# Prompt attention on one NeuronCore: where the masks are added to the scores, and which operand of the compressed scores stands still

## Chip, core and metric

The kernel runs on one core of one Trainium2 chip. The metric is the time of one execution on the device in microseconds (us). An execution under the hardware profiler gives the trace; its times carry the argument.

## What is computed

One step of a hybrid decoder layer: a prompt of 1024 positions, and 8 sequences that each decode one token. One normalized input feeds three groups of heads: NSA attention (8 query heads of 64, 2 key/value heads, and three branches: compressed, selected, window), an RWKV-7 recurrence, and attention into 256 memory tokens. Their gated outputs go through one output projection. The change concerns the prompt's NSA attention, for which the reference says:

```python
def masked_softmax(s, mask):
    s = jnp.where(mask, s.astype(jnp.float32), -jnp.inf)
    m = jnp.max(s, axis=-1, keepdims=True)
    m = jnp.where(jnp.isfinite(m), m, 0.0)
    p = jnp.exp(s - m)
    return p / jnp.maximum(jnp.sum(p, axis=-1, keepdims=True), 1e-30)
...
    s = jnp.einsum('qghd,cgd->qghc', qg, ck) * SCALE
    valid = cend[None, :] <= qpos[:, None]
    p = masked_softmax(s, valid[:, None, None, :])
...
    mask = (kpos[None, :] <= qpos[:, None]) & (kpos[None, :] > qpos[:, None] - WINDOW) & (kpos[None, :] >= 0)
    p = masked_softmax(s, mask[:, None, None, :])
```

With 1024 positions the 16 selected blocks of 64 are all blocks, so the selected branch is plain causal attention. The window has 512 positions. The compressed branch has 63 keys, each over 32 rows at a stride of 16, and a query sees those that end at or before it.

## The kernel before

The program has three phases: projections, the recurrence and the tables of the prompt (0 to about 518 us), prompt attention (518 to 838), and the output projection with the NSA attention of the decoded tokens (838 to 1001). The change lies in the second; its tables are made in the first, in `prompt_cmp` (L1172).

Prompt attention takes the queries in 8 tiles of 128, from tile i = 7 down to tile 0. Tile i sees n1 = 128(i+1) keys. A **unit** (i, g, hp) is two heads of key/value group g. `attn_scores` (L1300) computes it for two branches: b = 0 (selected, all n1 keys) and b = 1 (window, the last five blocks of 128). Scores are products in a rounded float format with the keys split in a high and a low part (kh and kl), per piece of up to 512 keys, with the queries as the stationary operand (the weights). For i >= 4 ("split") every head has a PSUM tile p_s of its own, 1024 wide; for i < 4 two heads share one. There are 64 split heads and branches, and 64 others in 32 pairs.

- Masks: `add` (L1323) adds them on TensorE as identity products. `bmask` holds two 128x128 masks as weights, `identb` (a bf16 identity) is the other operand. The last 128 keys get the diagonal mask, and for split tiles the first block of the window gets another. There are 160 such products.
- VectorE then searches the row maximum, negated: nm (L1337 for one head, L1345 for two at a time). ScalarE computes exp(score + nm) from PSUM into SBUF, p, with the row sum (L1338, L1347). VectorE forms the factor fac (L1348, L1349), and GpSimd scales p by it (L1352).
- `pt_copy` transposes p by blocks on TensorE (p_pT), and ScalarE and VectorE take turns copying the result to SBUF (pt, L1296 and L1298). `attn_out` multiplies by the values into p_o (L1385 takes it into cat).

`attn_cmp` (L1241) does the compressed branch once per tile: for each g the 64-column compressed keys ckh and ckl stand still and 512 query columns (4 heads) move; a mask cmask goes in by identb; ScalarE copies the result (sc, L1253); four transposes (p_sq) turn it, so that queries lie on the partitions; then VectorE and ScalarE do the softmax (pcq, L1261 to L1273) and pcq is transposed for the values.

**Order.** The program is written out in one order: scores of a unit are issued two units ahead of their use. Side work (queries of the next tile, memory attention, the decoded tokens' RWKV step in `sample_rwkv`) is woven between the steps. A modelled clock on TensorE's instructions paces it: every matmul and transpose adds its modelled time (a mask product adds 0.118 us), each side step states when it may go on, and each tile has a rate:

```python
        us = max(n, 256) * 4.6e-4 if x.dtype != F32 else max(n, 64) * 1.7e-3
        self.clock += us * self.rows / 128
...
            def slot():
                for j in (3, 2, 1, 0):
                    spent[j] = min(spent[j] + rate[j], 3.0)
                    while spent[j] >= 1 and self.te.clock >= ready[j]:
                        step(j)
```

PSUM has two p_s tiles, three tiles that p_pT, p_q, p_sc and p_sq share, and one p_o. p has buffers for two units. SyncE issues nearly all transfers.

Of the kernel before, what the change touches and what calls it, by code (L numbers as in the profile page):

```python
# [23 lines left out]
NEG = -1.0e30  # L24
# [24 lines left out]
def bc(ap, shape):  # L49
    return ap.to_broadcast(shape)  # L50
# [64 lines left out]
class Step:  # L115
# [1004 lines left out]
    def key_pools(self):  # L1120
        tc = self.tc
        self.kctx = ExitStack()
        R = lambda c, name, bufs: c.enter_context(tc.tile_pool(name=name, bufs=bufs, reuse_waits="tile", side="right"))
        self.catp = R(self.octx, "catp", 1)
        self.k1p = R(self.octx, "keys1", 1)
        self.kh, self.kl, self.vs = [], [], []
        self.cs2 = R(self.octx, "cs2", 1)
        self.key_tiles(R(self.kctx, "keys0", 1))
        self.key_tiles(self.k1p)
        self.kt = R(self.kctx, "keyst", 1)  # L1130
        self.ckh = self.kt.tile([128, 1, 128], F32R, name="ckh")
        self.ckl = self.kt.tile([128, 1, 128], F32R, name="ckl")
        self.cvk = self.kt.tile([128, 2, 64], F32, name="cvk")
        self.bmask = self.kt.tile([128, 2, 128], BF, name="bmask")
        self.identb = self.kt.tile([128, 128], BF, name="identb")
        self.qs, self.pcT, self.y_rw, self.turn, self.cat = {}, {}, {}, 0, {}

    def key_tiles(self, pool):
# [33 lines left out]
    def prompt_cmp(self):  # L1172
        nc, I, O = self.nc, self.I, self.O
        V, A, G, PE = nc.vector, nc.scalar, nc.gpsimd, nc.tensor
        am = self.wk.tile([128, 256], F32, name="c_am", tag="sc")
        nc.sync.dma_start(am[:], I["c_at"][:, 0:256])
        V.tensor_copy(self.bmask[:].rearrange("p a b -> p (a b)"), am[:])
        V.tensor_copy(self.identb[:], self.ident[:])
        self.cmask = self.kt.tile([128, 8, 128], BF, name="cmask")
        am = self.slot(4, [128, 1024], F32, "c_am")  # L1180
        nc.sync.dma_start(am[:], I["c_at"][:, 256:1280])
        V.tensor_copy(self.cmask[:].rearrange("p i c -> p (i c)"), am[:])
# [118 lines left out]
    def attn_scores(self, i, g, hp, Ps):  # L1301
# [9 lines left out]
        sm = self.small.tile([128, 2, 2], F32, name="sm")  # L1311

        def scores(ps, q, b, c0, c1):
            w = c1 - c0
            masks = [(w - 128, 0)] if c1 == n1 else []
            if b == 1 and split and c0 == w0:
                masks.append((0, 1))
            u, o = c0 // 512, c0 % 512
            PE.matmul(ps, q, self.kh[u][:, 2 * b + g, o:o + w], start=True, stop=False)
            PE.matmul(ps, q, self.kl[u][:, 2 * b + g, o:o + w], start=False, stop=not masks)  # L1320
            return [(ps[:, o:o + 128], m, k == len(masks) - 1) for k, (o, m) in enumerate(masks)]

        def add(masks):  # L1323
            for ps, m, stop in masks:
                PE.matmul(ps, self.identb[:], self.bmask[:, m, :], start=False, stop=stop)

        f = self.small.tile([128, 2, 2], F32, name="fac")
        hd = 4 * g + 2 * hp
        for b in range(2):
            c0 = w0 if b else 0  # L1330
            for h in range(2):
                Ps[h, b] = self.pp.tile([128, 1024 if b == 0 else 640], F32, name="p", tag=f"p{b}")
            if split:
                for h in range(2):
                    ps = self.pS.tile([128, 1024], F32, name="p_s", tag="s")
                    add(scores(ps[:, c0:512], qs[:, hd + h, :], b, c0, 512) + scores(ps[:, 512:n1], qs[:, hd + h, :], b, 512, n1))
                    V.tensor_reduce(nm[:, h, b:b + 1], ps[:, c0:n1], axis=AX.X, op=OP.max, negate=True)  # L1337
                    A.activation(Ps[h, b][:, :n1 - c0], ps[:, c0:n1], AF.Exp, bias=nm[:, h, b:b + 1],  # L1338
                                 accum_out=sm[:, h, b:b + 1])
# [9 lines left out]
            V.reciprocal(f[:, :, b], f[:, :, b])  # L1349
# [265 lines left out]
    def sample_setup(self):  # L1615
# [683 lines left out]
def host_consts():  # L2299
# [73 lines left out]
```

## Time and profile before

| | us |
|---|---|
| median of 3 runs | 1003.12 (1000.74 to 1004.17) |
| the profiled execution | 1003.45, span of the trace 1001.1, granted TensorE clock 0.991 |
| ScalarE: exponents L1338, 64 | 55.7, mean 873 ns |
| VectorE: reduces L1337, 64 | 57.6, mean 918 ns |
| VectorE: reduces L1345, 32 | 25.6 |
| GpSimd: scaling L1352, 128 | 211.5, mean 1666 ns |
| TensorE: mask products, 160 | 25.9, mean 0.16 a product |
| ScalarE: copies L1253 of compressed scores, 16 | 9.4, mean 589 ns |

A row of groups names a line, an engine, an operation, what it writes and reads, and a count; then busy time, mean duration, and the engine's idle time ahead of it with what ended it. On TensorE matmuls overlap, and their ends are modelled, so what one costs is read between the starts of its neighbours. The prediction below shows the rows that it uses.

### The profile page before, as it was taken

How to read it: one execution, taken by the hardware profiler on the slowest of the kernel's cores; microseconds unless marked ns; L12 is line 12 of the kernel's file. 1: busy time of each engine (PE TensorE's matmuls, PEld its weight loads, DVE VectorE, ACT ScalarE, POOL GpSimd, SP SyncE). 2: the span in 40 equal slices, each digit the busy share in tenths (PEclk: the TensorE clock that was granted, in tenths of full speed). 3: DMA queues.
4: the chain of work that ended last, by engine and by line, in shares of the span. 5: the costliest groups of instructions: out<-in, count | busy, mean ns of one | idle time of the engine just before them, and what ended most of it. 6: DMA issues, size and time to landing. Idle time of an engine off the chain costs nothing.

```text
span 1001.1 us, 24786 instructions
## 1 busy us (share of the span) xinstructions
PE 948.8 (95%) x9955; PEld 788.9 (79%) x9955; DVE 681.4 (68%) x1954; ACT 446.8 (45%) x1005; POOL 254.0 (25%) x221
## 2 busy tenths in 40 slices
PE   7999999999999998999987999999999988998997
PEld 7998888878887887788865777887878876877874
DVE  6759589756684997633548677676869986357364
ACT  6754224223522432224436656665476665224212
POOL 2000000000000000000008776766578853112010
PEclk9999999999999999999999999999999999999999
DMA  8321313212321162265255223411200064984412
GB/s 283 95 75 40 90 34 117 76 45 74 85 77 34 49 178 67 61 158 135 81 159 171 86 81 116 149 43 45 59 22 16 28 149 130 324 276 160 158 65 76
DMA packets 133978, 104.20 MB, mean 104 GB/s; under 512 B 34593, under 2 KB 121128, under 8 KB 133736
## 3 DMA queue, kind: packets, MB, share of 16 engines
q1 hardware_dynamic: 128904, 90.92, 30.8%
q0 software_dynamic: 3200, 10.49, 3.0%
q8 instruction: 78, 1.28, 0.5%
q10 hardware_dynamic: 1760, 1.21, 0.4%
q14 instruction: 36, 0.29, 0.1%
HBM read 84.00 MB, written 22.78 MB: 107 GB/s over the span
## 4 chain that ended last, share of the span: by engine, by line
PE 65%; DVE 18%; ACT 6%; issue 4%; DMA 3%; POOL 2%; SPq 2%; ACTq 0%; DVEq 0%; POOLq 0%
PE p_pr L87 20%; PE p_pr L284 8%; PE p_out L87 5%; PE p_s L87 4%; PE p_pT L87 4%; PE p_o L87 3%; ACT p L1338 2%; POOL p L1352 2%; PE p_iy L87 2%; DVE nm L1337 1%; PE p_hid L87 1%; PE p_z L87 1%; PE p_it L87 1%; ACT p L1347 1%; DVE pt L1298 1%
## 5 line engine op out<-in xcount | busy, mean ns | idle before, releaser
L1352 POOL TENSOR_SCALAR p<-p,fac 128x640 f32<-128x640 f32 (+7 forms) x128 | 211.5, 1666 | 89.6 <-DVE fac L1349 34.6
L87 PE MATMUL p_pr<-h,whi 128*128 128x512 f32 (+5 forms) x928 | 231.0, 340 | 0.3 <-issue 0.3
L87 PEld LDWEIGHTS p_pr<-h,whi 128*128 128x128 f32 (+1 forms) x928 | 147.3, 184 | 19.0 <-issue 3.0
L87 PE MATMUL p_pr<-h,wlo 128*128 128x512 f32 (+5 forms) x464 | 152.5, 329 | 0.0
L999 POOL MEMSET w2d<- 128x128 f32 x1 | 0.2, 205 | 399.8 <-PE p_yy L87 399.8
L87 PEld LDWEIGHTS p_pr<-h,wlo 128*128 128x128 f32 (+1 forms) x464 | 85.1, 183 | 9.7
L284 PE MATMUL p_pr<-h,whi 128*128 128x256 f32 (+2 forms) x416 | 88.3, 308 | 0.4 <-DVE h L233 0.4
L87 PE MATMUL p_pT<-ident,p 128*128 128x128 f32 x528 | 72.8, 280 | 7.0 <-POOL p L1352 3.5
L87 PE MATMUL p_s<-kh,qs 128*128 128x512 f32 (+3 forms) x191 | 71.1, 380 | 1.9 <-ACT p L1338 1.8
L87 PEld LDWEIGHTS p_pT<-ident,p 128*128 128x128 f32 x528 | 56.8, 140 | 19.6 <-issue 7.1
L87 PE MATMUL p_o<-pt,vs 128*64 128x128 f32 x1056 | 70.0, 282 | 1.1 <-DVE c_r L1272 0.7
L1338 ACT ACTIVATE p<-p_s,nm 128x640 f32<-128x640 f32 (+3 forms) x64 | 55.7, 873 | 32.6 <-DVE nm L1337 26.2
L284 PEld LDWEIGHTS p_pr<-h,whi 128*128 128x128 f32 x416 | 67.4, 192 | 3.6 <-DVE h L233 0.6
L1337 DVE TENSOR_REDUCE nm<-p_s 128x1 f32<-128x640 f32 (+3 forms) x64 | 57.6, 918 | 14.9 <-PE p_s L87 14.9
L274 DVE TENSOR_TENSOR wlo<-wraw,whi 128x1024 fp32r<-128x1024 f32 (+1 forms) x34 | 40.7, 1197 | 35.2 <-ACT whi L273 35.1
L87 PEld LDWEIGHTS p_o<-pt,vs 128*64 128x64 f32 x1056 | 59.0, 140 | 6.7 <-issue 2.7
L284 PE MATMUL p_pr<-h,wlo 128*128 128x256 f32 (+2 forms) x208 | 63.3, 306 | 0.0
L87 PE MATMUL p_s<-kl,qs 128*128 128x512 f32 (+3 forms) x192 | 61.7, 338 | 0.0
L273 ACT ACTIVATE whi<-wraw 128x1024 fp32r<-128x1024 f32 (+1 forms) x35 | 36.4, 1039 | 50.9 <-PE p_pr L87 36.8
L1298 DVE COPY pt<-p_pT 128x512 f32<-128x512 f32 (+1 forms) x72 | 47.8, 670 | 16.2 <-PE p_pT L87 15.9
L1296 ACT ACTIVATE pt<-p_pT 128x512 f32<-128x512 f32 (+1 forms) x72 | 42.1, 587 | 27.6 <-PE p_pT L87 27.2
L87 PE MATMUL p_out<-woh,chi 128*128 128x512 f32 x128 | 52.5, 410 | 0.8 <-ACT woh L2194 0.6
(539 smaller groups left out, 2005.2 us busy)
## 6 DMA issues: line engine op xcount, KB each, us to landing
wraw<-in_w_in_dram SPq DMA_DIRECT2D x34, 512.0 KB
pg<-in_c_pool_dram SPq DMA_DIRECT2D x40, 256.0 KB
pg<-in_c_pool_dram SPq DMA_DIRECT2D x48, 128.0 KB
x<-in_x_prompt_dram SPq DMA_DIRECT2D x8, 512.0 KB
z_d<-zt SPq DMA_DIRECT2D x16, 256.0 KB
cat<-z_d SPq DMA_DIRECT2D x8, 512.0 KB
xres<-in_x_prompt_dram POOLq DMA_DIRECT2D x16, 256.0 KB, 3.8
wor<-in_w_out_dram SPq DMA_DIRECT2D x16, 256.0 KB
```

The lines of the kernel that those rows point to most:

```text
L87: self.last = getattr(self.engine, op)(*a, **k)
L273: nc.scalar.activation(hi[:, :, :n], raw[:, :, :n], AF.Copy)
L274: (low or nc.vector).tensor_tensor(lo[:, :, :n], raw[:, :, :n], hi[:, :, :n].bitcast(F32), op=OP.subtract)
L284: self.last_mm = self.pe.matmul(ps[:m, :b - a], w[:, k, :m], h[k][:, a:b], start=(k == 0 and i == 0), stop=(k == 7 and i == 2))
L999: nc.gpsimd.memset(w2d[:], 0.0)
L1296: nc.scalar.activation(pt[:, :n], ps[:, :n], AF.Copy)
L1298: nc.vector.tensor_copy(pt[:, :n], ps[:, :n])
L1337: V.tensor_reduce(nm[:, h, b:b + 1], ps[:, c0:n1], axis=AX.X, op=OP.max, negate=True)
L1338: A.activation(Ps[h, b][:, :n1 - c0], ps[:, c0:n1], AF.Exp, bias=nm[:, h, b:b + 1], accum_out=sm[:, h, b:b + 1])
L1347: A.activation(Ps[h, b][:, :n1], ps[:, h, :n1], AF.Exp, bias=nm[:, h, b:b + 1], accum_out=sm[:, h, b:b + 1])
L1352: nc.gpsimd.tensor_scalar(x, x, f[:, h, b:b + 1], None, op0=OP.mult)
```

## The change

`weigh` takes the place of the identity products, of the reduces and of ScalarE's reading of PSUM. bmask is now one row of masks, 128x1152: an "after" block, 896 columns of zeros and the diagonal block. Its last w columns are the mask of w keys; two pieces of 320 at a distance of 832 make the window's mask. One VectorE operation per head writes -(score + mask) to p in SBUF and keeps the row's minimum, which is the negated maximum; ScalarE then takes the exponent in place with scale -1.

```diff
-                    add(scores(ps[:, c0:512], qs[:, hd + h, :], b, c0, 512) + scores(ps[:, 512:n1], qs[:, hd + h, :], b, 512, n1))
-                    V.tensor_reduce(nm[:, h, b:b + 1], ps[:, c0:n1], axis=AX.X, op=OP.max, negate=True)
-                    A.activation(Ps[h, b][:, :n1 - c0], ps[:, c0:n1], AF.Exp, bias=nm[:, h, b:b + 1],
-                                 accum_out=sm[:, h, b:b + 1])
+                    scores(ps[:, c0:512], qs[:, hd + h, :], b, c0, 512)
+                    scores(ps[:, 512:n1], qs[:, hd + h, :], b, 512, n1)
+                    weigh(ps[:, c0:n1], h, b, c0)
...
-                add([m for h in range(2) for m in scores(ps[:, h, :n1], qs[:, hd + h, :], b, 0, n1)])
-                V.tensor_reduce(nm[:, :, b], ps[:, :, :n1], axis=AX.X, op=OP.max, negate=True)
                 for h in range(2):
-                    A.activation(Ps[h, b][:, :n1], ps[:, h, :n1], AF.Exp, bias=nm[:, h, b:b + 1], accum_out=sm[:, h, b:b + 1])
+                    scores(ps[:, h, :n1], qs[:, hd + h, :], b, 0, n1)
+                for h in range(2):
+                    weigh(ps[:, h, :n1], h, b, 0)
...
+        def weigh(ps, h, b, c0):
+            x, w = Ps[h, b][:, :n1 - c0], n1 - c0
+            if b == 1 and split:
+                m = bass.AP(tensor=self.bmask.tensor, offset=self.bmask.offset, ap=[self.bmask.ap[0], [832, 2], [1, 320]])
+                halves = lambda t: t.rearrange("p (a c) -> p a c", a=2)
+            else:
+                m, halves = self.bmask[:, 1152 - w:1152], lambda t: t
+            V.tensor_tensor_reduce(halves(x), halves(ps), m, -1.0, 3.0e38, op0=OP.add, op1=OP.min, accum_out=nm[:, h, b:b + 1])
+            A.activation(x, x, AF.Exp, scale=-1.0, bias=nm[:, h, b:b + 1], accum_out=sm[:, h, b:b + 1])
```

In `attn_cmp` the queries of one head stand still, and 64 compressed keys of one group move: 16 products into one PSUM tile that has queries on its partitions from the start, after one product that adds the mask for all heads. The copies sc and the transposes p_sq are gone.

```diff
-        for g in range(2):
-            pc = self.pM.tile([128, 4, 128], F32, name="p_sc", tag="m")
-            for n, ck in enumerate((self.ckh, self.ckl)):
-                PE.matmul(pc[:], ck[:, 0, :], qs[:, 4 * g:4 * g + 4, :], start=(n == 0), stop=False)
-            PE.matmul(pc[:], self.identb[:], bc(self.cmask[:, i:i + 1, :], [128, 4, 128]), start=False, stop=True)
-            A.activation(sc[g * 64:(g + 1) * 64], pc[g * 64:(g + 1) * 64], AF.Copy)
-            yield 0.5 + 2 * g
-        p2 = self.pM.tile([128, 4, 2, 64], F32, name="p_sq", tag="m")
+        p2 = self.pM.tile([128, 4, 2, 64], F32, name="p_sc", tag="m")
+        x = 56 - 8 * i
+        PE.matmul(p2[:].rearrange("p a b c -> p (a b) c"), self.cmask[:, 120:248],
+                  bc(self.cmask[:, None, x:x + 64], [128, 8, 64]), start=True, stop=False)
         for j in range(4):
-            PE.transpose(p2[:, j].rearrange("p g c -> p (g c)"), sc[:, j, :], self.ident[:])
+            for g in range(2):
+                for n, ck in enumerate((self.ckh, self.ckl)):
+                    PE.matmul(p2[:, j, g], qs[:, 4 * g + j, :], ck[:, 0, g * 64:g * 64 + 64], start=False, stop=(j == 3 and g == 1 and n == 1))
+            if j == 1:
+                yield 0.1
```

The tables follow: one transfer of 128x504 instead of 128x256 and 128x1024, GpSimd clears bmask, VectorE casts three pieces, identb is gone. In `sample_setup` the reciprocal root takes its memory from another pool.

```diff
-        r = self.rsqrt(self.small, ps[:, 0:64], 64, 1.0 / 64, 1e-6)
+        r = self.rsqrt(self.we, ps[:, 0:64], 64, 1.0 / 64, 1e-6)
```

Three places show how instructions move. First TensorE in tile 5, around the compressed scores. Before, two masks per window score and the mask of the compressed scores each load identb:

```order
L87 MATMUL p_s<-kh_6305,qs 128x256
L87 MATMUL p_s<-kl_6306,qs 128x256
L87 MATMUL p_s<-kh_6308,qs 128x384
L87 MATMUL p_s<-kl_6309,qs 128x384
L87 LDWEIGHTS identb
L87 MATMUL p_s<-bmask,identb 128x128
L87 LDWEIGHTS identb
L87 MATMUL p_s<-bmask,identb 128x128
L87 MATMUL p_sc<-qs,ckh 128x512
L87 MATMUL p_sc<-qs,ckl 128x512
L87 LDWEIGHTS identb
L87 MATMUL p_sc<-cmask,identb 128x512
```

In the changed kernel, at the place of tile 5's compressed scores:

```order
L87 MATMUL p_sc<-ckh,qs 128x64
L87 MATMUL p_sc<-ckl,qs 128x64
L87 MATMUL p_s<-kh_6305,qs 128x512
L87 MATMUL p_s<-kl_6306,qs 128x512
L87 MATMUL p_s<-kh_6308,qs 128x384
L87 MATMUL p_s<-kl_6309,qs 128x384
L87 MATMUL p_sc<-ckh,qs 128x64
L87 MATMUL p_sc<-ckl,qs 128x64
```

The scores of heads now follow one another without masks (these are the 896 keys of tile 6), and the compressed products stand in two runs of eight between them.

Second, VectorE in tile 2's scores, around the start of the recurrence's long operations (L2136 before, L2133 now), before (nm is the negated maximum, rw_a belongs to the decoded tokens' recurrence, qhl to the next queries, pt is a copied transpose):

```order
L2136 TENSOR_TENSOR rw_a_10311<-rw_a_10311,rw_a_10312 128x1024
L1345 TENSOR_REDUCE nm<-p_s 128x2 x2
L1228 TENSOR_TENSOR qhl<-q,qhl 128x4x64
L2138 TENSOR_TENSOR rw_a_10311<-rw_a_10311,rw_a_10312 128x1024
L1348 SCALAR_TENSOR_TENSOR fac<-sm,gates 128x2 x2
L1385 TENSOR_TENSOR cat_10279<-cat_10279,p_o 128x128
```

In the changed kernel:

```order
L1322 ISA p,nm<-p_s,bmask 128x384
L1322 ISA nm 128x1
L1322 ISA p,nm<-p_s,bmask 128x384
L1322 ISA nm 128x1
L1382 TENSOR_TENSOR cat_10197<-cat_10197,p_o 128x128
L1226 TENSOR_TENSOR qhl<-q,qhl 128x4x64
L1345 SCALAR_TENSOR_TENSOR fac<-sm,gates 128x2
L2135 TENSOR_TENSOR rw_a_10229<-rw_a_10229,rw_a_10230 128x1024
```

The two reduces of 2 x 384 columns have become four fused operations of 384 (a row that writes p and nm), each followed by an instruction that writes nm alone; the rows above are the last two of the four, and ahead of the four stands the recurrence's first long operation, as before. The next one, L2135, stands behind the product into cat, a step later than before, and the ones after it slip further.

Third, SyncE where the third phase begins, before (cat and w1a are operands of the end of phase 2 and of phase 3, wor the output weights, v_new the new rows of the decoded tokens):

```order
L1239 DMA cat_11567<-z_d 128x8x128
L961 DMA w1a<-in_cmp_w_dram 128x8x64 x4
L2192 DMA wor<-in_w_out_dram 128x512 x3
L1883 DMA v_new<-out_dram 32x2x128 x4
L2192 DMA wor<-in_w_out_dram 128x512 x5
```

In the changed kernel:

```order
L1855 DMA pg<-in_c_pool_dram 128x256
L1237 DMA cat_11429<-z_d 128x8x128
L961 DMA w1a<-in_cmp_w_dram 128x8x64 x4
L1880 DMA v_new<-out_dram 32x2x128 x4
L2189 DMA wor<-in_w_out_dram 128x512 x8
```

The reads of v_new have moved past three loads of output weights.

More of the change, by code (lines that the diff above doesn't have):

```diff
@@ L1133, in key_pools @@
         self.cvk = self.kt.tile([128, 2, 64], F32, name="cvk")
-        self.bmask = self.kt.tile([128, 2, 128], BF, name="bmask")
-        self.identb = self.kt.tile([128, 128], BF, name="identb")
+        self.bmask = self.kt.tile([128, 1152], BF, name="bmask")
         self.qs, self.pcT, self.y_rw, self.turn, self.cat = {}, {}, {}, 0, {}
@@ L1174, in prompt_cmp @@
         V, A, G, PE = nc.vector, nc.scalar, nc.gpsimd, nc.tensor
[L1175 to L1182, printed above, removed]
+        am = self.slot(4, [128, 504], F32, "c_am")
+        nc.sync.dma_start(am[:], I["c_at"][:, 0:504])
+        G.memset(self.bmask[:], 0.0)
+        V.tensor_copy(self.bmask[:, 0:128], am[:, 128:256])
+        V.tensor_copy(self.bmask[:, 1024:1152], am[:, 0:128])
+        self.cmask = self.kt.tile([128, 248], F32R, name="cmask")
+        V.tensor_copy(self.cmask[:], am[:, 256:504])
         self.load_w1([self.slot(e, [128, 8, 2, 64], F32, f"w1s{e}") for e in range(2)])
@@ L1246, in attn_cmp @@
         gate = self.gates[:, i, :].rearrange("p (h b) -> p h b", b=3)
-        sc = self.we.tile([128, 4, 128], F32, name="sc", tag="sc")
-        for g in range(2):
-            pc = self.pM.tile([128, 4, 128], F32, name="p_sc", tag="m")
-            for n, ck in enumerate((self.ckh, self.ckl)):
-                PE.matmul(pc[:], ck[:, 0, :], qs[:, 4 * g:4 * g + 4, :], start=(n == 0), stop=False)
-            PE.matmul(pc[:], self.identb[:], bc(self.cmask[:, i:i + 1, :], [128, 4, 128]), start=False, stop=True)
-            A.activation(sc[g * 64:(g + 1) * 64], pc[g * 64:(g + 1) * 64], AF.Copy)
-            yield 0.5 + 2 * g
-        p2 = self.pM.tile([128, 4, 2, 64], F32, name="p_sq", tag="m")
-        for j in range(4):
-            PE.transpose(p2[:, j].rearrange("p g c -> p (g c)"), sc[:, j, :], self.ident[:])
+        p2 = self.pM.tile([128, 4, 2, 64], F32, name="p_sc", tag="m")
+        x = 56 - 8 * i
+        PE.matmul(p2[:].rearrange("p a b c -> p (a b) c"), self.cmask[:, 120:248],
+                  bc(self.cmask[:, None, x:x + 64], [128, 8, 64]), start=True, stop=False)
+        for j in range(4):
+            for g in range(2):
[3 more added lines that the diff above has]
+                yield 0.1
         pcq = self.we.tile([128, 8, 64], F32, name="pcq", tag="pcq")
@@ L1313, in scores @@
         def scores(ps, q, b, c0, c1):
[L1314 to L1318, printed above, removed]
-            PE.matmul(ps, q, self.kh[u][:, 2 * b + g, o:o + w], start=True, stop=False)
[L1320 to L1325, printed above, removed]
+            u, o, w = c0 // 512, c0 % 512, c1 - c0
+            PE.matmul(ps, q, self.kh[u][:, 2 * b + g, o:o + w], start=True, stop=False)
+            PE.matmul(ps, q, self.kl[u][:, 2 * b + g, o:o + w], start=False, stop=True)
+        def weigh(ps, h, b, c0):
[7 more added lines that the diff above has]
+            A.activation(x, x, AF.Exp, scale=-1.0, bias=nm[:, h, b:b + 1], accum_out=sm[:, h, b:b + 1])
         f = self.small.tile([128, 2, 2], F32, name="fac")
@@ L2320, in host_consts @@
         rw[h * 64:(h + 1) * 64, 416 + h] = 1.0
-    at = np.zeros((128, 1280), np.float32)
+    at = np.zeros((128, 504), np.float32)
     kq = np.arange(128)[None, :]
@@ L2324, in host_consts @@
     at[:, 128:256] = np.where(kq > p[:, None], 0.0, NEG)
-    c = p[:, None] % 64
-    at[:, 256:1280] = np.where((16 * c + 31 <= np.arange(1024)[None, :]) & (c < 63), 0.0, NEG)
+    y = np.arange(120)[None, :] - 55
+    at[:, 256:376] = np.where(p[:, None] == np.minimum(y, 8), NEG, 0.0)
+    at[:, 376:504] = np.where((kq < 16 * p[:, None] + 15) & (p[:, None] < 9), 1.0, 0.0)
     dc = np.zeros((128, 320), np.float32)
```

## Prediction

> **What bounds the kernel now.** I read the page first: TensorE's share and the chain that ended last.
>
> ```profile
> span 1001.1 us, 24786 instructions
> PE 948.8 (95%) x9955; PEld 788.9 (79%) x9955; DVE 681.4 (68%) x1954; ACT 446.8 (45%) x1005; POOL 254.0 (25%) x221
> PE 65%; DVE 18%; ACT 6%; issue 4%; DMA 3%; POOL 2%; SPq 2%; ACTq 0%; DVEq 0%; POOLq 0%
> ```
>
> TensorE is busy for 95% and holds 65% of the chain; VectorE holds 18%. These are averages. The change lies in prompt attention, 518 to 838 us, so I cut that stage by its tiles: start-up (tile 7's first unit), tiles 7 to 4, tile 3, most of tiles 2 to 0, the rest, and phase 3. The view of busy time by stretch gives, after each window and its length, the busy us (and instructions) of PE, PEld, DVE, ACT, POOL, then the granted clock, the DMA share and GB/s.
>
> ```profile
> 518.00:560.00 42.00, 34.87 (x271) 25.28 (x271) 31.84 (x74) 25.84 (x58) 32.25 (x17) 0.96 0.55 169
> 560.00:728.00 168.00, 161.74 (x1637) 133.82 (x1635) 122.55 (x293) 102.48 (x243) 109.81 (x60) 0.99 0.27 82
> 728.00:750.00 22.00, 21.70 (x199) 17.06 (x198) 14.85 (x29) 15.63 (x40) 17.17 (x11) 1.00 0.06 19
> 750.00:810.00 60.00, 58.18 (x615) 49.83 (x612) 57.05 (x136) 42.16 (x123) 49.81 (x39) 1.00 0.14 41
> 810.00:838.00 28.00, 23.09 (x233) 19.19 (x233) 18.84 (x63) 12.45 (x48) 12.16 (x19) 0.94 0.43 101
> 838.00:1001.00 163.00, 148.90 (x952) 114.81 (x946) 90.01 (x227) 47.79 (x87) 21.85 (x41) 0.99 0.55 180
> ```
>
> From 560 to 750 TensorE is full (161.74 of 168, 21.70 of 22) and VectorE is not (122.55, 14.85): work taken from TensorE shortens these stretches. From 750 to 810 **both** are full: 58.18 and 57.05 of 60. There whatever VectorE gains in work is added to the time, and what TensorE loses is worth nothing. At start-up and from 810 neither is full; latency decides.
>
> **Mask products removed (TensorE).** The same windows for the mask tile alone: length, PE busy (count), DVE busy (count), clock.
>
> ```profile
> 518.00:560.00 42.00, 3.66 (x20) 0.00 (x0) 0.96 0.55 169
> 560.00:728.00 168.00, 12.94 (x76) 0.00 (x0) 0.99 0.27 82
> 728.00:750.00 22.00, 1.71 (x12) 0.00 (x0) 1.00 0.06 19
> 750.00:810.00 60.00, 5.14 (x36) 0.00 (x0) 1.00 0.14 41
> 810.00:838.00 28.00, 2.44 (x16) 0.00 (x0) 0.94 0.43 101
> ```
>
> Matmuls overlap, so the price is read between starts, not from these busy times. Two pieces of TensorE's timeline (start, us, instruction):
>
> ```profile
> 625.01 0.28 PE L87 MATMUL p_s<-kl,qs 128*128 128x256 f32 x1
> 625.12 0.23 PE L87 MATMUL p_s<-bmask,identb 128*128 128x128 bf16 x1
> 625.16 0.47 PE L87 MATMUL p_s<-kh,qs 128*128 128x512 f32 x1
> 625.48 0.39 PE L87 MATMUL p_s<-kl,qs 128*128 128x512 f32 x1
> ...
> 645.98 0.47 PE L87 MATMUL p_sc<-qs,ckh 128*128 128x512 f32 x1
> 646.30 0.40 PE L87 MATMUL p_sc<-qs,ckl 128*128 128x512 f32 x1
> 646.53 0.39 PE L87 MATMUL p_sc<-cmask,identb 128*128 128x512 bf16 x1
> 646.57 0.53 PE L87 MATMUL p_s<-kh,qs 128*128 128x384 f32 x1
> 646.94 0.34 PE L87 MATMUL p_s<-kl,qs 128*128 128x384 f32 x1
> 647.11 0.28 PE L87 MATMUL p_s<-kh,qs 128*128 128x256 f32 x1
> 647.23 0.28 PE L87 MATMUL p_s<-kl,qs 128*128 128x256 f32 x1
> 647.35 0.29 PE L87 MATMUL p_s<-bmask,identb 128*128 128x128 bf16 x2
> 647.57 0.64 PE L87 MATMUL p_wo<-wxv,s_pT 128*32 128x128 f32 x16
> ```
>
> A matmul of 256 columns holds TensorE for 0.12 us (647.11 to 647.23), one of 512 for 0.23 (646.30 to 646.53). From kl at 625.01 to kl at 625.48 lie 0.47 us where those two would take 0.35: 0.12 for one mask. The pair at 647.35 delays what follows from 647.35 to 647.57: 0.11 each. What follows a group loads new weights anyway, so part of that lag stays; I take **0.09 us each**, with bounds 0.04 (625.12 to 625.16, the mask's own step) and 0.12. That is 20, 76, 12, 36 and 16 times 0.09 = 1.8, 6.8, 1.1, 3.2 and 1.4 us, 14.3 in all (6.4 to 19.2).
>
> **The search for the maximum (VectorE).** Groups by shape: busy us, mean ns, idle before; then one row of the windows for L1345 (after the length: DVE busy and count), two rows of VectorE's timeline, and ScalarE's read of its sum.
>
> ```profile
> L1337 DVE TENSOR_REDUCE nm<-p_s 128x1 f32<-128x640 f32 x40 | 32.2, 818 | 10.7 <-PE p_s L87 10.7
> L1263 DVE TENSOR_TENSOR pcq<-p_sq,c_m 128x512 f32<-128x512 f32 x8 | 5.5, 684 | 0.1
> L1407 DVE TENSOR_TENSOR pmem<-pmem,sm_m 128x512 f32<-128x512 f32 x16 | 11.7, 732 | 0.3
> L1385 DVE TENSOR_TENSOR cat<-cat,p_o 128x128 f32<-128x128 f32 x31 | 8.7, 281 | 6.0 <-PE p_o L87 6.0
> ...
> 750.00:810.00 60.00, 15.14 (x18) 1.00 0.14 41
> ...
> 772.23 0.22 DVE L1349 RECIPROCAL fac<-fac 128x2 f32<-128x2 f32 x2
> 772.36 1.20 DVE L2140 TENSOR_REDUCE rw_a<-rw_a 128x16 f32<-128x1024 f32 x1
> ...
> L1338 ACT ACTIVATION_READ_ACCUMULATOR p<-p_s,nm 128x1 f32 x64 | 12.6, 197 | 0.0
> ```
>
> The fused operation reads scores from PSUM and the mask from SBUF. [...] New is the second instruction that reads the accumulator out, one per head. No row of VectorE shows it. From below: two tiny reciprocals at 772.23 let the next start at 772.36, about 0.07 us each; from above ScalarE's read, 0.197. I take **r = 0.10 us**, nearer to VectorE's own tiny operations. Where i < 4, one reduce over two heads becomes two operations, another 0.07 each.
>
> [...] L1407 with both inputs in SBUF takes 732, 0.05 more than L1263. So I put no contention into the sum and 0.05 into the upper bound. [...]
>
> By stretch:
> - 518 to 560: 14 heads times 0.10 in a chain of latencies, against 1.8 on TensorE. The exponent now reads SBUF, so the score tile comes free after the search instead of after the exponent; that shortens the waits in this row:
>
> ```profile
> PE p_s L87 <- ACT p L1338: 1.8, 2, 1.0
> ```
>
>  I take 2.0 us less (4 less to 1 more).
> - 560 to 728: 50 heads, 5 us more on VectorE, 127.6 of some 161: covered, except where a copy of transposed weights stands behind it on VectorE and TensorE waits. 6.8 less 0.3 = **6.5 less**. Without cover the 5 us would come back.
> - 728 to 750: 12 heads, 1.2 + 6 x 0.07 = 1.6 more, 16.5 of 21: covered. 1.1 less.
> - 750 to 810: the 18 reduces become 36: 3.6 + 18 x 0.07 = 4.9 more on VectorE. Of its 2.95 idle I let half be used: 4.9 - 1.5 = **3.4 more, taken as 3.5**; the 3.2 off TensorE bring nothing.
> - 810 to 838: 16 heads, 1.6 + 8 x 0.07 = 2.2 more, a third of it in the chain, against 1.4: 0.7 less.
>
> **Compressed scores.** Before, a group of 512 columns costs 645.98 to 646.57 plus the 0.20 by which the next kh at 646.57 is long (0.37 against 0.17 for 384 columns): 0.79, twice a tile, plus four transposes, which change weights each time. So do the sixteen new matmuls of 64 columns. The price of a change of weights:
>
> ```profile
> 622.10 1.53 PE L87 MATMUL p_pT<-ident,p 128*128 128x128 f32 x12
> 623.54 0.44 PE L87 MATMUL p_moT<-ident,m_o 128*128 128x128 f32 x2
> ```
>
> Twelve in 1.44 us: 0.12 each. Before 1.58 + 0.48 = 2.06 a tile, after 16 x 0.12 + 0.23 = 2.15: 8 tiles, 0.7 more; the two copies on ScalarE and the trip through them go. I take 0.3 more (2 less to 3 more).
>
> **Covered edits.** ScalarE has 42 of 60 and 102 of 168 us busy, and loses two copies a tile: an exponent that reads SBUF may cost it some tens of ns more or less; without that cover 0.05 each is 6 us. The mask load becomes one transfer, and the clearing on GpSimd stands in phase 1, long before tile 7. The sample's reciprocal root only changes its memory pool.
>
> **Moved.** The modelled clock that paces the side work no longer counts the mask products, so side steps come later in program order; most lie on engines with room, and some VectorE work leaves 750 to 810 for the stretch behind, which has 9 us of room. On SyncE's queue the four reads of v_new now stand ahead of all eight output weight loads, not behind three:
>
> ```profile
> 836.00 1.30 SPq L2192 DMA_DIRECT2D wor<-in_w_out_dram  x3
> 838.96 1.74 SPq L1883 DMA_DIRECT2D v_new<-out_dram  x4
> ```
>
> The first three weights can be late by up to 1.7 plus v_new's wait, the other five are earlier by 1.3. I take 0.5 more (1.5 less to 2 more).
>
> Sum: -2.0 - 6.5 - 1.1 + 3.5 - 0.7 + 0.3 + 0.5 = **-6.0**. The profiled execution took 1003.45 us, 0.3 over the median of the runs, a difference I neglect: **997.5 us**.
>
> **Rivals.**
> - VectorE keeps up. If r is near 0.07, side work leaves 750 to 810, and TensorE's 3.2 us count there too: -2 - 6.8 - 1.1 - 3.2 - 1.4 = -14.5, about 989. For it: 560 to 750 has room. Against it: 57.05 of 60.
> - Given back. Side steps that come later meet the latency-bound stretch from 810 and the weight loads behind it; 4 to 6 us of the gain return: 1002.5. For it: the last stretch has 28 us with only 23 of TensorE, so a late chain is not hidden.
> - VectorE becomes the bound. At an extra x = 0.25 a head (read-out 0.20, contention 0.05): 750 to 810 gains 36 x 0.25 + 1.3 - 1.5 = 8.8; 560 to 728 keeps 6.8 - 0.2 x 12.5 = 4.3; start-up 0; 728 to 750 -0.6; 810 to 838 half of 4.6 less 1.4 = +0.9; +0.8 of the rest: +5.6, 1009. Between x = 0.10 (-6) and 0.25 (+5.6) it decides from x about 0.18 on.
> - Half rate. If the fused operation took two cycles a column, 750 to 810 alone would gain 15.14 - 18 x 0.15 = 12.4 on top of 3.5, 560 to 728 some 36 us of VectorE (163 of 161), start-up 6: about 1030. L1263 speaks against it. [...]
> - The change doesn't do what it says: TensorE's stalls merely move from masks to the copies behind VectorE, and 560 to 728 stays at 168. Time: 1003.
>
> **How the numbers follow.** Forecast 0.44, own range 993 to 1001; VectorE keeps up 0.16; given back 0.12; stalls only moved 0.06; VectorE bound or late weights 0.18; half rate 0.04. Below 0.3% (3 us) a measurement of this kernel cannot tell a difference from none. Faster: 0.40 of the forecast, the 0.16, 0.04 of given back: 0.60. Same: the rest of the forecast and of given back, and the stalls that only move: 0.18. Slower: 0.22. The range takes in 989 and 1009 and leaves out the half rate and the outer parts: 988 to 1009.
>
> **What would show it.** Rows of 160 mask products gone, matmuls in 560 to 728 denser and that stretch some 6 us shorter; the read-out's spacing on VectorE near 0.1; VectorE at 60 or more in what was 750 to 810, and that stretch longer. A read-out of 0.2, a fused operation over 0.85 us at 640 columns, or an output projection that starts later would make me wrong.

## The result, and the profile after

The change is **slower** by 0.8%: 1008.02 us (median of 7 runs, 1007.04 to 1011.59) against 1000.56 for the kernel before (7 runs, 998.48 to 1004.17); ratio 1.0077, 95% interval 1.0055 to 1.0099. The prediction was 997.5, with a range from 988 to 1009: the sign was wrong.

The page of the changed kernel (busy us and share; then its chain):

```profile
span 1006.3 us, 24739 instructions
PE 942.7 (94%) x9851; PEld 793.3 (79%) x9851; DVE 680.5 (68%) x2114; ACT 442.9 (44%) x989; POOL 252.6 (25%) x222
PE 26%; DVE 9%; ACT 5%; issue 2%; DMA 2%; SPq 2%; POOL 1%; ACTq 0%; DVEq 0%; POOLq 0%
```

The chain breaks off early here (its shares add up to under half), so it isn't used. Busy time by stretch, columns as before:

```profile
518.00:560.00 42.00, 33.55 (x259) 26.83 (x259) 31.62 (x84) 25.43 (x56) 31.77 (x17) 0.92 0.52 158
560.00:728.00 168.00, 158.08 (x1587) 133.84 (x1586) 119.87 (x344) 100.12 (x235) 111.22 (x60) 0.98 0.27 82
728.00:750.00 22.00, 21.07 (x190) 17.38 (x187) 15.97 (x52) 15.92 (x39) 16.36 (x12) 1.00 0.06 20
750.00:810.00 60.00, 56.69 (x593) 50.03 (x591) 56.69 (x186) 40.68 (x121) 48.68 (x39) 1.00 0.13 37
810.00:838.00 28.00, 19.38 (x182) 16.75 (x183) 18.84 (x90) 11.44 (x45) 10.01 (x17) 0.79 0.49 127
838.00:1001.00 163.00, 151.82 (x973) 118.52 (x970) 88.83 (x223) 48.87 (x89) 22.62 (x42) 0.97 0.54 177
```

Two columns changed that the prediction didn't look at: TensorE's idle time from 560 to 728 grew from 6.3 to 9.9 us, and its granted clock fell in four of the six stretches, from 810 to 838 from 0.94 to 0.79. TensorE's longest waits from 560 to 850, before and then after (total us, times, longest):

```profile
PE p_sy L87 <- ACT p L1347: 2.2, 1, 2.2
PE p_pT L87 <- POOL p L1352: 2.0, 5, 0.8
PE p_q L87 <- DVE pt L1298: 1.6, 1, 1.6
```

```profile
PE p_sy L87 <- issue: 6.7, 1, 6.7
PE p_wS L87 <- DVE wkt L1802: 3.9, 1, 3.9
PE p_pT L87 <- DVE cat L1429: 2.0, 1, 2.0
...
PE p_o L87 <- DVE sm_m L1403: 1.1, 1, 1.1
```

None of the four waits for the search or the exponent of the prompt's scores. p_sy, at 810, turns the result of the decoded tokens' recurrence (rw_a). The view names no releaser for it, but VectorE's last operation on rw_a ends at 817.01 and p_sy starts at 817.11 (814.07 and 814.18 before). TensorE was free for it at 810.45, where before it was at 811.98: of the 4.5 us that this wait grew, 1.5 come from an early TensorE and 2.9 from a late operand. p_wS, at 655, are the decoded tokens' window scores against their keys (wkt). The third, at 598, waits behind a VectorE instruction that waits for a load of such keys.

p_wS waits for one column of the keys that VectorE copies in. Before, the last two of these copies ran ahead of a tile's compressed softmax (which began at 653.01); now they stand behind it. First the row of before, then two of now:

```profile
652.09 0.20 DVE L1805 COPY wkt<-s_o 128x1 f32<-128x1 f32 x2
...
652.95 0.69 DVE L1258 TENSOR_REDUCE c_m<-p_sc 128x8 f32<-128x512 f32 x1 [0.18 <-PE p_sc L87]
658.31 0.21 DVE L1802 COPY wkt<-s_o 128x1 f32<-128x1 f32 x2
```

Around p_sy, in pieces of 5 us (columns as above; the last three are clock, DMA share and GB/s):

```profile
810.00:815.00 5.00, 0.45 (x4) 0.30 (x3) 4.71 (x25) 2.30 (x9) 2.72 (x5) 0.77 0.66 204
815.00:820.00 5.00, 2.89 (x22) 2.57 (x24) 2.18 (x8) 0.60 (x1) 0.05 (x1) 0.50 0.60 152
820.00:825.00 5.00, 5.00 (x46) 4.56 (x43) 2.39 (x12) 1.54 (x6) 0.00 (x0) 0.71 0.82 167
825.00:830.00 5.00, 5.00 (x64) 4.63 (x61) 3.67 (x22) 2.95 (x13) 3.91 (x7) 1.00 0.00 2
...
835.00:840.00 5.00, 3.10 (x24) 2.35 (x26) 2.10 (x10) 0.53 (x3) 0.59 (x1) 0.66 0.56 160
840.00:845.00 5.00, 4.91 (x52) 4.00 (x49) 1.67 (x7) 3.15 (x5) 0.60 (x1) 0.66 0.00 0
```

The wait is paid twice: TensorE is idle for 6.7 us, and then it works at a granted clock of 0.50 until 823. Read in steps of 1 us, the granted clock falls to 0.50 in **spells of 3.4 us**, each worth 1.7 us of lost work, one to five in a row.

That gives an account from tile 7's first score product to the start of the third phase (p_new). Waits are gaps between matmuls, long ones over 0.8 us; the loss by clock is the sum of (1 - clock) over the time, less what fell into waits; work is what is left.

| us | length | long waits | short waits | lost by clock | work at full clock |
|---|---|---|---|---|---|
| before | 320.9 | 10.3 | 10.1 | 5.1 | 295.4 |
| the change | 328.3 | 19.7 | 11.9 | 12.2 | 284.5 |
| difference | +7.4 | +9.4 | +1.8 | +7.1 | -10.9 |

TensorE did lose some 11 us of work, and 18 came back as waits and half clock. By place:

| us | before | the change | predicted difference |
|---|---|---|---|
| to the end of tile 7's first unit | 35.8 | 35.2 | -2.0 |
| from there to the end of tile 2's last unit (802.30, 799.62) | 248.6 | 248.6 | -4.1 (-6.5 - 1.1 + 3.5) |
| from there to p_new | 36.5 | 44.5 | -0.2 (-0.7 + 0.5) |

(The 0.3 more for the compressed scores was spread over all tiles.) In the middle stretch TensorE has 7.2 us less work (238.9 and 231.7) and takes the same time; the loss itself lies in the last one, where p_sy waits.

**Where the load of the window keys went.** SyncE's timeline from 565 to 599, before and after:

```profile
565.05 1.26 SPq L1744 DMA_DIRECT2D mxv<-in_cache_mem_dram  x2
577.24 0.36 SPq L1741 DMA_DIRECT2D mkt<-in_c_memk_dram  x1
577.64 1.38 SPq L1804 DMA_DIRECT2D wkt<-in_c_wink_dram  x3
579.07 0.58 SPq L1803 DMA_DIRECT2D out_dram<-in_cache_win_dram  x1
598.30 0.33 SPq L1222 DMA_DIRECT2D q<-q_d  x1
```

```profile
568.11 1.26 SPq L1741 DMA_DIRECT2D mxv<-in_cache_mem_dram  x2
592.24 0.35 SPq L1220 DMA_DIRECT2D q<-q_d  x1
592.68 0.38 SPq L1738 DMA_DIRECT2D mkt<-in_c_memk_dram  x1
593.11 0.89 SPq L1801 DMA_DIRECT2D wkt<-in_c_wink_dram  x2
```

The load of the next queries (q) waits for its buffer, which GpSimd's qhl frees. Before, it stood behind the keys; in the change's order it stands ahead of them, and the keys are asked for 15 us later. The clock that leaves out the masks doesn't do this alone: in e2 below, which has that clock, the keys go at 581.32 and q at 601.97. On VectorE a copy of one column then waits for them, with scores queued behind it:

```profile
592.44 0.69 DVE L1295 COPY pt<-p_pT 128x512 f32<-128x512 f32 x1
597.58 0.15 DVE L1802 COPY wkt<-s_o 128x1 f32<-128x1 f32 x1 [4.45 <-DMA wkt<-in_c_wink_dram]
597.73 1.09 DVE L1322 CUSTOM_DVE_ANT_0 p<-p_s,bmask 128x896 f32<-128x896 f32 x1
598.74 0.08 DVE L1322 DVE_READ_ACCUMULATOR2_ANT nm<- 128x1 f32 x1
```

VectorE's new instructions themselves, by shape (busy us, mean ns):

```profile
L1322 DVE CUSTOM_DVE_ANT_1 p<-p_s,bmask 128x640 f32<-128x640 f32 x32 | 25.4, 818 | 4.8 <-PE p_s L87 4.6
...
L1322 DVE DVE_READ_ACCUMULATOR2_ANT nm<- 128x1 f32 x128 | 10.4, 81 | 0.0
```

The fused operation over 640 columns took what the reduce did (818 ns), and the read-out 81 ns, inside the bounds and under the value taken.

### The profile page after: what moved, and what is told of

Its sections match the earlier page's. It is cut to its first block, busy times and chain, and to the rows that moved or that the text cites. A ratio compares the mean times of both kernels' runs of the same rounds, so it can differ in the third digit from the quotient of the medians.

```text
span 1006.3 us, 24739 instructions
## 1 busy us (share of the span) xinstructions
PE 942.7 (94%) x9851; PEld 793.3 (79%) x9851; DVE 680.5 (68%) x2114; ACT 442.9 (44%) x989; POOL 252.6 (25%) x222
## 5 line engine op out<-in xcount | busy, mean ns | idle before, releaser
L1349 POOL TENSOR_SCALAR p<-p,fac 128x640 f32<-128x640 f32 (+7 forms) x128 | 208.8, 1647 | 92.6 <-DVE fac L1346 33.0
L1323 ACT ACTIVATE p<-p,nm 128x640 f32<-128x640 f32 (+7 forms) x128 | 93.1, 728 | 63.5 <-DVE nm L1322 59.7
L87 PE MATMUL p_pT<-ident,p 128*128 128x128 f32 x528 | 74.9, 287 | 11.5 <-POOL p L1349 5.9
L87 PEld LDWEIGHTS p_pT<-ident,p 128*128 128x128 f32 x528 | 58.9, 144 | 24.3 <-issue 9.9
L1322 DVE CUSTOM_DVE_ANT_0 p<-p_s,bmask 128x512 f32<-128x512 f32 (+7 forms) x96 | 60.1, 662 | 14.7 <-PE p_s L87 10.2
L87 PE MATMUL p_s<-kh,qs 128*128 128x512 f32 (+3 forms) x191 | 66.3, 359 | 0.9 <-DVE nm L1322 0.9
L87 PE MATMUL p_out<-wol,chi 128*128 128x512 f32 x128 | 51.3, 401 | 1.1 <-DVE wol L2192 1.0
```

The costliest lines, as they stand in the source:

```text
L87: self.last = getattr(self.engine, op)(*a, **k)
L1322: V.tensor_tensor_reduce(halves(x), halves(ps), m, -1.0, 3.0e38, op0=OP.add, op1=OP.min, accum_out=nm[:, h, b:b + 1])
L1323: A.activation(x, x, AF.Exp, scale=-1.0, bias=nm[:, h, b:b + 1], accum_out=sm[:, h, b:b + 1])
```

## The experiments

Theories: **stall** (the loss is waits that the new order exposes, and the half clock behind them), **engine** (VectorE's added instructions), and the **compressed scores**. Times are ratios to runs of the kernel before on the same chip, with a 95% interval.

### The pace alone, and each half of the change

e1: the change, with the clock still counting the masks.

```diff
             PE.matmul(ps, q, self.kl[u][:, 2 * b + g, o:o + w], start=False, stop=True)
+            PE.clock += 256 * 4.6e-4 * ((c1 == n1) + (b == 1 and split and c0 == w0))
```

> The change with the modelled clock still counting 0.118 us for each removed mask product, so that side work is written out by the old pace. Against 1000.6 us before and 1008.0 of the change: if the change loses because side work lands at other places and exposes its chains (pace theory), 996 to 1001; if VectorE's added instructions cost it (engine theory), 1006 to 1009; if the compressed scores cost it, 1006 to 1009.

e2: the kernel before, masks not counted.

```diff
                 PE.matmul(ps, self.identb[:], self.bmask[:, m, :], start=False, stop=stop)
+                PE.clock -= 256 * 4.6e-4
```

> The kernel before, mask products and all, with a modelled clock that doesn't count them. Nothing is added to or taken from any engine. Pace theory: 1004 to 1008. Engine theory and compressed-scores theory: 1000 to 1002.

e3: the change with the compressed scores of before (its mask product in the new float format).

```diff
-                    PE.matmul(p2[:, j, g], qs[:, 4 * g + j, :], ck[:, 0, g * 64:g * 64 + 64], start=False, stop=(j == 3 and g == 1 and n == 1))
+                PE.matmul(pc[:], ck[:, 0, :], qs[:, 4 * g:4 * g + 4, :], start=(n == 0), stop=False)
...
+            PE.transpose(p2[:, j].rearrange("p g c -> p (g c)"), sc[:, j, :], self.ident[:])
```

> The change with the compressed scores done as before (keys stationary, copies and transposes), masks on VectorE. Pace theory: 1004 to 1009, since the pace is as in the change. Engine theory: 1006 to 1009. Compressed-scores theory: 998 to 1001.

e4: the reverse, the kernel before with the new compressed scores.

```diff
-                PE.matmul(pc[:], ck[:, 0, :], qs[:, 4 * g:4 * g + 4, :], start=(n == 0), stop=False)
+                    PE.matmul(p2[:, j, g], qs[:, 4 * g + j, :], ck[:, 0, g * 64:g * 64 + 64], start=False, stop=(j == 3 and g == 1 and n == 1))
```

> The kernel before with the new compressed scores alone (queries stationary), masks on TensorE. Pace theory and engine theory: 999 to 1002. Compressed-scores theory: 1005 or more.

| | ratio | interval |
|---|---|---|
| e1 pace kept | 1.0067 | 1.0041 to 1.0092 |
| e2 pace less | 1.0099 | 1.0071 to 1.0127 |
| e3 masks only | 1.0214 | 1.0185 to 1.0243 |
| e4 compressed scores only | 1.0041 | 1.0022 to 1.0060 |

e2 is the telling one: nothing moved between engines, only the order was written by another clock, and it costs 1%. Its p_wS waits 3.8 us. But e1 misses its forecast. The cause lay in my edit: the compressed scores too add to the clock, and have one yield fewer, so e1 is in a third order. Two pairs share TensorE's order exactly: e1 with e4, and e2 with e3. In both, taking the masks off TensorE gained nothing (1.0041 to 1.0067; 1.0099 to 1.0214). e3 lies above all three of its forecasts, e4 between its two. But the kernel ties TensorE's instructions to the written order and not the other engines', and the other queues differ within a pair: in e1 SyncE issues q at 599.05, ahead of the keys at 599.93, in e4 the keys at 581.88, ahead of q at 597.73. So the pairs don't isolate VectorE's work. In e3 the waits are long:

```profile
PE p_wS L87 <- DVE wkt L1805: 9.7, 3, 4.6
PE p_sy L87 <- issue: 4.5, 1, 4.5
PE p_sm L87 <- DVE pt L1298: 4.4, 1, 4.4
PE p_pTm L87 <- DVE fac L1348: 2.7, 1, 2.7
```

### The old order, and the two late chains mended

e5 adds to e1 the clock and the yields of the old compressed scores; TensorE's order of all else is then that of before, row for row; SyncE's and VectorE's are not (the third load of keys goes at 595.04, before at 578.64).

```diff
+        t = PE.clock
...
+            if j % 2:
+                PE.clock = t + 3 * 512 * 4.6e-4
+                yield 0.5 + j - 1
+                t = PE.clock
+        PE.clock += 4 * 0.11
```

> The change with TensorE's order of everything but masks and compressed scores as it was before, row for row. Ratio to before. If the loss comes from the new order on the queues (stall theory): 0.985 to 0.998, since masks then leave TensorE and no load has moved. If it comes from VectorE's added work in the score chain (engine theory): 1.002 to 1.010.

e6: the change, with q loaded by GpSimd's queue (there the wait is for GpSimd's own earlier instruction).

```diff
-        nc.sync.dma_start(q[:].rearrange("p h d -> p (h d)"), self.q_d[i * 128:(i + 1) * 128, :])
+        (nc.sync if first else nc.gpsimd).dma_start(q[:].rearrange("p h d -> p (h d)"), self.q_d[i * 128:(i + 1) * 128, :])
```

> The change with the loads of the next tile's queries issued by GpSimd instead of SyncE; TensorE's order stays. The window keys then no longer queue behind a query load that waits for its buffer. Stall theory: the waits at 598 (2.0 us) and 655 (3.9) and the two spells of half clock behind them (1.7 each) go, about 9 us off the change's 1.0077: 0.997 to 1.002. Engine theory: 1.006 to 1.010.

e7: the change, with p_sy written later.

```diff
-        yield from wait(6.0)
+        yield from wait(14.0)
         py = self.pM.tile([128, 2, NS], F32, name="p_sy", tag="m")
```

> The change with the two transposes p_sy written 8 modelled us later; nothing else moves on TensorE. Stall theory: the wait of 6.7 us at 810 shrinks to under 1, and the half clock behind it, 7 to 9 us off: 0.998 to 1.002. Engine theory: the wait only moves to the next instruction that needs VectorE, 1.006 to 1.010.

e8: both edits.

> The two edits together. Stall theory: the savings add, 0.988 to 0.996, faster than both kernels. Engine theory: 1.005 to 1.010.

| | ratio | interval |
|---|---|---|
| the change | 1.0077 | 1.0055 to 1.0099 |
| e5 old order | 1.0031 | 1.0012 to 1.0049 |
| e6 q on GpSimd | 1.0005 | 0.9986 to 1.0025 |
| e7 p_sy later | 0.9963 | 0.9943 to 0.9983 |
| e8 both | 0.9922 | 0.9896 to 0.9947 |

In e6 the keys are asked for at 579 again and the wait at 598 is gone; p_wS still waits 3.9, against the forecast, since its copies still stand behind the softmax. In e7 the p_sy wait is gone, and so are the three spells behind it; the last stretch of the account shrinks from 44.5 to 35.6 us. Together they turn 0.8% slower into 0.8% faster. e5 came out in the range of the engine theory and misses that of the stall theory (0.985 to 0.998). Its trace shows that TensorE in the old order met **other** waits, also in the score chain (p behind GpSimd), so TensorE's order alone isn't the cause either:

```profile
PE p_pT L87 <- POOL p L1354: 5.2, 8, 1.8
PE p_sy L87 <- issue: 3.3, 1, 3.3
PE p_sh L87 <- DVE s_x L1652: 3.2, 1, 3.2
PE p_pT L87 <- ACT pt L1297: 2.6, 7, 0.6
PE p_sl L87 <- ACT rw_b L2077: 2.6, 1, 2.6
```

### What of this is the change's own

e9: the kernel before with both edits. e10: e5 with both.

> The kernel before (masks on TensorE, old compressed scores) with the two edits of the run that won: query loads on GpSimd, p_sy 8 modelled us later. Ratio to before. Stall theory: only the wait of 2.2 us at 812 and the half clock behind it (1.7) can go, 0.995 to 0.999; so 0.3 to 0.7% of the winner's 0.9922 is the change's own. If the two edits alone make the winner: 0.990 to 0.994.

> The change in the old order (1.0031) with the two edits. Stall theory: the wait of 3.4 us for p_sy and 1.7 to 3.4 of half clock go, 0.996 to 0.999; if the old order's loss came from VectorE, 1.002 to 1.004.

e11: e8 with the second p_wS later.

```diff
+            if a:
+                yield 6.0
             ps = self.pM.tile([128, 512], F32, name="p_wS", tag="m")
```

> The winner with the second scores of the window branch of the decoded tokens (p_wS) 6 modelled us later, past the wait of 3.9 us that is left at 652. Stall theory: 3.9 + 1.7 off if nothing new waits, 0.986 to 0.990; engine theory: 0.991 to 0.994.

e12: e8 with two more tiny VectorE instructions behind each read-out.

```diff
+            for k in range(2):
+                V.tensor_copy(ex[:, h, b:b + 1], nm[:, h, b:b + 1])
             A.activation(x, x, AF.Exp, scale=-1.0, bias=nm[:, h, b:b + 1], accum_out=sm[:, h, b:b + 1])
```

> The winner with two more VectorE instructions of 128x1 behind each of the 128 read-outs (copies nobody reads), so three times the read-out's price; TensorE's order stays. Engine theory, VectorE the bound from 750 to 810: 36 x 0.15 = 5 us and more, 0.998 to 1.003. Stall theory, VectorE covered: under 2 us, 0.991 to 0.995.

| | ratio | interval | median us |
|---|---|---|---|
| e9 before, both edits | 0.9943 | 0.9918 to 0.9967 | 999.30 |
| e10 old order, both edits | 0.9951 | 0.9932 to 0.9969 | 1000.38 |
| e11 e8, p_wS later | 0.9910 | 0.9884 to 0.9936 | 996.34 |
| e12 more read-outs | 1.0012 | 0.9990 to 1.0035 | 1005.43 |

e9 misses on the low side: the kernel before, too, gains 0.6% from the edits, so most of e8's gain isn't the change's. e10, a little under its forecast, is no faster than e9: in TensorE's old order the change is then worth nothing. e11 against e9, same chip: 3.0 us, the best that the change showed, though the two intervals overlap. e11 also misses in part: the p_wS wait went and a wait of 2.5 us for another transpose came in its place. e12 came out on the side of the engine theory in its time, but its trace doesn't show VectorE as the bound from 750 to 810. The longest waits of e12:

```profile
PE p_sy L87 <- DVE rw_a L2177: 3.8, 1, 3.8
PE p_wS L87 <- DVE wkt L1805: 2.9, 1, 2.9
```

The added instructions delayed the recurrence's small operations on VectorE, p_sy waits again, and three spells of half clock (5.1 us) stand behind it; between the ends of tile 7's first and tile 2's last unit e12 is only 1.3 us longer than e8 (246.3 against 245.0), though VectorE has 256 instructions more. So work added to VectorE does cost time, some 9 us here, through a late operand and not through a full engine. (VectorE's order also differs between e8 and e12.)

### TensorE's work alone, and a stall put in

e16 adds nothing to VectorE and drops the mask products from e9, with the clock still counting them, so that TensorE's order stays. The prompt's scores are then unmasked. VectorE has the same instructions, in another order in some places.

```diff
             for ps, m, stop in masks:
-                PE.matmul(ps, self.identb[:], self.bmask[:, m, :], start=False, stop=stop)
+                PE.clock += 256 * 4.6e-4
```

> The kernel before with the two edits and without the 160 mask products (the diagonal and window masks are left out of the prompt's scores); VectorE keeps its plain reduces, TensorE's order is otherwise that of the kernel before. Ratio to before; with the products it was 0.9943. If new stalls come from TensorE alone, which now reaches the same waits earlier: 0.991 to 0.996. If the change's gain was lost on VectorE's added instructions: 0.980 to 0.986.

Measured 0.9917 (0.9890 to 0.9943), against 0.9943 (0.9918 to 0.9967) with the products: 2.6 us, by the two intervals anything from nothing to some 6. By the account above its work at full clock is 282.0 us, 13.3 less than e9's 295.3; long waits rose from 6.7 to 16.1, the loss by clock from 3.4 to 10.2. (The traced execution is a long one, 1002.64 us where the median is 997.72; its middle stretch is 2.0 us shorter than e9's.) So of 160 products, 13 us of TensorE's work, at least half comes back, with nothing at all added elsewhere:

```profile
PE p_sh L87 <- DVE s_x L1650: 3.2, 1, 3.2
PE p_pT L87 <- POOL p L1352: 2.7, 4, 2.0
PE p_o L87 <- DVE cat L1385: 2.4, 2, 2.0
PE p_sl L87 <- ACT rw_b L2075: 2.2, 1, 2.2
```

p_sh and p_sl are the same new waits as in e5: operands of the decoded tokens that come from chains of small operations. TensorE reaches p_sh 2.1 us earlier than in e9 (545.19 and 547.33) and it isn't ready earlier (548.40); it reaches p_sl 3.1 us earlier (701.70 and 704.84), and that is ready only 1.6 earlier (703.89 and 705.49). e10 has the same order on TensorE and the change's work on VectorE besides: it is 3.4 us slower than e16. Part of this are the new compressed scores, with which e4's work is 297.6 us, 2.2 more than before.

e13, e14 and e15 put one stall into e9, in tile 5, where TensorE is full. n is 8, 16 and 32.

```diff
+        self.te.matmul(p[:], self.ident[:], self.ident[:, 0:8], start=True, stop=True)
+        self.nc.vector.tensor_copy(x[:], p[:])
+        for k in range(n):
+            self.nc.vector.tensor_scalar(y[:], x[:], 1.0, None, op0=OP.add)
+            x, y = y, x
...
+        self.te.matmul(p[:], self.ident[:], x[:], start=True, stop=True)
```

> The kernel before with the two edits, and one stall put into a full stretch of TensorE (tile 5, near 668 us): a tiny matmul waits for 8 small VectorE operations in a chain, about 2 us. If a stall brings half clock behind it: a spell of 3.4 us at half clock within 5 us behind the stall, or none if 2 us is too short; if the half clock comes by itself, none.

> The same with 16 operations, about 4 us. If a stall brings half clock: at least one spell of 3.4 us (1.7 lost) right behind it, so that TensorE is some 5.5 us later in all. If not: 4 us.

> The same with 32 operations, about 8 us. If a stall brings half clock: two or three spells (3.4 to 5.1 lost, part of it within the stall itself). If not: 8 us.

| | TensorE idle, us | half clock behind or in it, us lost | unit ends later than in e9 by, us |
|---|---|---|---|
| e13 | 3.35 | 3.4 | 7.0 |
| e14 | 4.99 | 3.4 | 8.4 |
| e15 | 8.28 | 5.1 | 11.2 |

The stalls came out longer than meant (a step of the chain takes 0.2 us and the way in and out some 2). The last column is the time from the end of the unit ahead of the stall to the end of the next, against e9's 11.9. e14 in pieces of 2 us:

```profile
668.00:670.00 2.00, 0.00 (x0) 0.00 (x0) 1.75 (x8) 0.00 (x0) 1.04 (x1) 1.00 0.00 0
670.00:672.00 2.00, 0.52 (x3) 0.55 (x3) 1.13 (x7) 0.00 (x0) 0.00 (x0) 0.54 0.00 0
672.00:674.00 2.00, 2.00 (x8) 1.61 (x8) 0.47 (x2) 0.00 (x0) 0.00 (x0) 0.50 0.00 0
674.00:676.00 2.00, 2.00 (x11) 1.48 (x9) 1.44 (x2) 0.99 (x2) 0.00 (x0) 0.50 0.00 0
676.00:678.00 2.00, 2.00 (x26) 1.83 (x26) 1.09 (x4) 0.99 (x2) 0.12 (x1) 0.75 0.00 0
```

The stall ends at 671.5, full clock is back at about 677. In e9 no spell stands there. So the stall brings the half clock, and in these three executions, one of each kernel, 3.35 us or more of idle time in a full stretch cost twice over: the idle time and about 3 us more.

## Why the prediction was wrong

- **"From 560 to 750 TensorE is full: work taken from TensorE shortens these stretches."** This is the first step that failed. Its size was about right: I priced 14.3 us of masks, e16 shows 13.3, and the change loses 10.9 with the compressed scores (priced 0.7 more, e4 shows 2.2). But from tile 7's first unit to tile 2's last both kernels take 248.6 us. A full engine isn't the only limit: TensorE's queue is one list in which the score products stand between operands of other chains (the window keys, the recurrence, the small operations of the decoded tokens). With the products most of those were just in time; without them TensorE arrives early and waits (3.2 us for p_sh and 2.2 for p_sl in e16), or the operand itself comes later in VectorE's new order (the copies for p_wS). e16 shows that removing the products is enough to lose half or more of their 13 us; it doesn't separate the early TensorE from VectorE's changed order.
- **"I take 0.5 more" for what is moved, and 0.7 less from 810 on.** This is the second step that failed, and the larger: the last stretch is 8.0 us longer. I followed v_new past the output weights, and said of the side steps only that they come later. What counted there was p_sy, whose operand ends 2.9 us later and whose wait brings three spells of half clock; e7 takes both away and measures 1.1%. The other move was q ahead of wkt on SyncE. It was to be seen in the order of that queue, and the trace before had the price: q issues at 598.30, where the keys went at 577.64. e6 measures it at about 0.7%, of which its trace accounts for 4.1 us (the stage of the account takes 324.2 instead of 328.3). The two together save 1.6%.
- **No term for the half clock.** The row of before from 810 to 838 had 0.94 for the clock behind a wait of 2.2 us; I quoted it and didn't ask why. The change lost 7.1 us more by it, beside 9.4 by longer waits. In its trace the spells of 3.4 us at a clock of 0.50 stand at the waits: one behind an idle time of 2.0 us (at 598), one behind 3.9 (at 655), three from within 6.7 (at 810), and two from within one of 1.1 (at 836). How much idle time brings a spell, and what ends one, the runs don't show.
- **"VectorE becomes the bound"** gave 1009, near the result, by a mechanism that wasn't at work; that the range reached so far and holds 1008.02 is luck. x was 0.08 a head, not 0.25. From tile 3's first to tile 2's last unit, the ends lie 44.8 us apart before (757.49 to 802.30) and 43.9 after (755.71 to 799.62), so the 3.5 us that I added for 750 to 810 weren't there; 56.69 of 60 for both engines, as after the change, is not a bound by itself. VectorE did cost time, but as the source of late operands (p_sy, p_wS).
- **"Given back"** was the nearest rival, at 1002.5 and 0.12: a place was named (a late chain in the last stretch), the price left out the half clock and the waits at 598 and 655.
- Right: the read-out, 81 ns, between 0.07 and 0.20. The sum has no term for a fused operation dearer than the reduce; that was my estimate, and no row of before shows the operation. The change shows it at 818 ns for 640 columns and 684 for 512, where the reduces of before took 818 and 679: no loss, no half rate, and no contention to be seen with a GpSimd that is busy for 111 of 168 us. The exponent that reads SBUF took 25 to 36 ns more than the one that reads PSUM (824 against 793 ns at 640 columns). The output projection starts later, which was named as a sign of being wrong: 848.08 instead of 842.72, the 5.3 us by which p_new is late (844.12 and 838.81); the third phase itself takes no longer.

Open: e8's wait for p_wS is left, and e11 only replaced it. Whether the 2.6 to 3.0 us that the change may be worth would grow with every chain mended wasn't tried. No run keeps VectorE's and SyncE's order with the masks on VectorE, so it isn't shown how much of p_sy's late operand comes from the fused operations and how much from the order. The start-up stretch lost between 1.7 and 10.2 us by clock from one profiled execution to another, which the runs don't explain; 1.2 of the account's 7.1 lie there.

## What to carry to other kernels

- Work taken from the busiest engine is worth only what the other operands in its queue allow: 13.3 us less on TensorE gave e16 2.6 us against e9, by their ratios. Before you count it, list what the engine waits for in that stretch, and when each of those would be ready if the engine came earlier by what you save.
- Where a modelled clock or a planner writes the order, an edit that changes its count is a second edit. Compare every queue's order, SyncE's and VectorE's above all: a load that waits for its buffer holds everything behind it (here q, asked for at 592.24, the window keys, 15 us later than before), and TensorE's order kept row for row (e5) didn't keep theirs.
- Keep the old order in one run and the old engines in another. e2 and e16 cost a line each, and separate much of what the whole change mixes.

## What the runs showed of the hardware

- In e13 to e15 a stall put into a full stretch cost TensorE its length and 2.9 to 3.7 us more: 3.35 us idle cost 7.0, 4.99 cost 8.4, 8.28 cost 11.2. The granted clock fell to 0.50 in spells of 3.4 us (1.7 lost each).
- From 560 to 850 us in the traces before and after, each of the four idle times of 2.0 us or more shows a spell within it or at most 1.6 us behind it: 2.20 us to 814.18 before (0.50 from 815.4), and in the change 2.02 to 600.18 (601.1), 3.86 to 658.51 (659.1) and 6.66 to 817.11 (from 812.7). So do those of 2.6 and 3.3 us in e5 (at 702 and 816), 2.6 in e10 (701), 3.8 in e12 (825) and 2.2 in e16 (701). Of two shorter ones, 1.07 us to 837.04 in the change had two from 836.6, and 1.63 to 689.11 before was followed by one only at 706. In the start-up of before, 2.25 us to 539.69 had none behind it up to 706.
- In the change VectorE's read-out of its accumulator took 81 ns (mean of 128); the fused add and minimum over 640 columns took 818 ns, the same as the plain reduce before.
